# Two blanked triangles of turned p, written straight onto their partitions, and loads placed by fixed leads, in a two-layer decoder trunk

## The chip, the cores and the metric

The kernel runs on one core of one Trainium2 chip. The time is device microseconds (us) of one launch, the median of several runs. The engines are called PE (TensorE matmul; PEld is its weight load), DVE (VectorE), ACT (ScalarE), POOL (GpSimd) and SP (SyncE, which here only issues DMAs).

## The reference

Two decoder layers on x of 1024 tokens by 1024 channels, float32. Layer 0 mixes tokens with a short gated convolution, layer 1 with sliding-window attention; each is followed by a dense SwiGLU channel mixer.

```python
def reference(x, ...):
    for i in range(DEPTH):
        h = rmsnorm(x, norm_mixer[i])
        if i % N_MIXERS == 0:
            mix = short_conv_mixer(h, conv_w_in[j], conv_w[j], conv_w_out[j])
        else:
            mix = swa_sink_attention(h, attn_w_qkv[j], attn_q_gain[j], attn_k_gain[j], attn_sinks[j], attn_w_o[j])
        x = x + mix
        h = rmsnorm(x, norm_ffn[i])
        x = x + swiglu_ffn(h, ffn_w_gate_up[i], ffn_w_down[i])
    return x
```

The attention has 16 query heads and 4 key/value heads of 64 channels, with query and key normed for each head, a distance bias and a sink for each head. It works in blocks of 128 queries. A query at place q of its block sees the keys j <= q of its own block and the keys j > q of the block before: 128 keys in all, so that the two masks fit together like two triangles of one square.

## The kernel before

Activations lie with the channel on the partitions. Every product is made from float32r halves: an operand is split into a high part and the rest (a low part), and three matmuls (high by high, high by low, low by high) stand for one float32 product. So PE does three matmuls for each block of a product, and ACT and DVE split the operands.

**The order is written out by hand.** A `Line` holds PE's work in order; `line.work(n, f)` puts in work of n matmuls of 0.2265 us (`MM`), and `line.at(t, f)` places the work of the other engines at a time t on that same planned clock. `line.run()` then issues everything in the order of these times. Each engine, and SP's queue too, works off its own instructions strictly in that order, so an instruction that waits holds up all that stand behind it on its engine. The planned times set only the order; when things really run is decided by the semaphores.

**The attention** runs through 32 units u = 0 to 31: block b = u // 4, and within it one key/value head with its four query heads (QUAD). While unit u's scores are made, unit u - 1 is turned (transposed) and unit u - 2 is multiplied by v. On POOL stand, for each unit, the `normal` of p (L1931), the blanking (`select`), a difference of v (`dv_sum`, `dv_lo`) and the low parts of the output (`o_lo`). The steps that the change touches:

- `merge`, `bias`, `least`, `exponents`, `inverse`, `normal`: one square of scores for each head, own block where j <= q and the block before where j > q, then the softmax in the room `e_room`.
- `turn` (L1937): four transposes give p with the keys on the partitions. `turn_hi` (ACT, L1948) and `turn_lo` (DVE, L1952) put its high and low part into a room w (tag G0).
- `values` (L1972): both parts times a mixed v, whose partitions 0 to 63 hold the own block and 64 to 127 the block before.
- The mixed v is wrong for two triangles of the square: keys 0 to 63 with j > q (first half of the queries), and keys 64 to 127 with j <= q (second half). `other_values` (L1981) puts them right: it multiplies the difference of the two v's (`dv_room`) with these triangles alone. Each matmul has 128 partitions, 64 keys with the high part of p and the same 64 keys with the low part.
- `select` (POOL, L1957 and L1958) blanks all but the triangle with `affine_select`, for the high part (e = 0) and the low part (e = 1), into a second room o (tag G1). It leaves both parts of a triangle on the partitions that they came from. `under` (SP, L1962 and L1963) then copies two of the four pieces to the other 64 partitions with two DMAs inside SBUF, 64 partitions by 256 elements each.

Both rooms are single: `select` of one unit waits until `other_values` of the unit before has read o.

**What else is on SP's queue.** `key_twice` (L1782), `v_down` (L1795) and `dv_twice` (L1811, L1812) are small DMAs inside SBUF. From unit 24 on, PE's free places are filled with the output projection (`tail_part`, L1061 to L1063), tiles m = 0 to 7 of the first half of the tokens, eight pieces of three matmuls each, then the same for the second half. Each tile loads its `w_o`, which an earlier stage has split and stored (`wo_parts`), as two DMAs of 512 KB (L1035) into a pair of rooms; three pairs take turns (WR, WH, WL). `load_again` (L2209) brings the residual tiles X0 to X7 back from `xmid`, 512 KB each; the rooms have held query weights until unit 26. The residual add (L1086) needs X of a tile when the tile is done. From the sums of squares that follow come the means (L1103).

Where these loads stand before: `state["loads"]` keeps, for each unit, a time 5.1 us behind its start. The `wo` loads of a tile stand at the last of these marks that is at least 7 us ahead of the tile, or 15 us ahead of it if that is later. X0 stands at the start of unit 27, and one further X near the mark of each unit from 27 to 33.

Of the kernel before, what the change touches and what calls it, by code (L numbers as in the profile page):

```python
# [11 lines left out]
F32R = mybir.dt.float32r  # L12
AF = mybir.ActivationFunctionType
ALU = mybir.AluOpType

P = 128
# [4 lines left out]
HD = 64  # L21
# [11 lines left out]
QUAD = NH // NKV  # L33
# [37 lines left out]
def trunk_kernel(ctx: ExitStack, tc: tile.TileContext, xT, small, table, w_in, w_out, w_kv, w_q, w_o, w_gu, w_dn, out):  # L71
    nc = tc.nc
    sb = ctx.enter_context(tc.tile_pool(name="sb", bufs=1))
    pm = ctx.enter_context(tc.tile_pool(name="pm", bufs=1, space=bass.MemoryType.PSUM))
    dve, act, pool, pe = nc.vector, nc.scalar, nc.gpsimd, nc.tensor
# [3 lines left out]
    def slot(tag, shape=(P, D), dtype=F32, bufs=1):  # L79
        uid[0] += 1  # L80
        return sb.tile(list(shape), dtype, tag=tag, name=f"{tag}_{uid[0]}", bufs=bufs)
# [28 lines left out]
    def plain(ap):  # L110
        return ap.bitcast(F32)
# [125 lines left out]
    state = {}  # L237
# [550 lines left out]
    class Line:  # L788
# [8 lines left out]
        def at(self, t, f, *args):  # L797
            self.n += 1
            heapq.heappush(self.heap, (t, self.n, f, args))
# [205 lines left out]
    def channel_mixer(layer, next_stage, src_of, operands, raw_tags, extra_tags, slots, line, lead_in):  # L1005

        at = line.at
# [10 lines left out]
        def tail_weights(h, m, t):  # L1018
            it = {}

            def load():
                it["w"] = Weights()
                it["w"].load(src_of(m), 0, n_op)

            def hi():
                c = slice(0, n_op * P)
                it["w"].alloc()
                it["steps"] = split_steps(it["w"].hi[:, c], it["w"].lo[:, c], it["w"].raw[:, c])
                it["steps"][0]()

            def load_parts():
                tag = ("WR", "WH", "WL")[(NK * h + m) % 3]
                it["w"] = SimpleNamespace(hi=slot(tag, dtype=F32R, bufs=2), lo=slot(tag, dtype=F32R, bufs=2))
                for e, room in enumerate((it["w"].hi, it["w"].lo)):
                    nc.sync.dma_start(plain(room), wo_parts[m][e])  # L1035

            if layer == 1:
                at(max([b for b in state["loads"] if b < t - 7.0][-1], t - 15.0), load_parts)
            else:
                at(t - 14.0, load)  # L1040
                at(t - 5.2, hi)
                at(t - 4.2, lambda: it["steps"][1]())
            return lambda: (it["w"].hi, it["w"].lo)
# [113 lines left out]
        for u in range(GROUP):  # L1157
            if whole:
                t = (origin + 4.0, origin + 12.0, begin1 + 1.0, begin1 + 8.0)[u]
# [12 lines left out]
        t = begin1 + 6.2  # L1172
        for odd in (0, 1):
            if odd and whole:
                t = begin1 + 28.0
# [5 lines left out]
        t = begin2 + 6.2  # L1181
# [30 lines left out]
        t = begin2 + 20.5  # L1212
# [309 lines left out]
        for k in range(1, KINDS):  # L1522
            s = begin + GROUP * down * k
# [14 lines left out]
        for k in range(1, KINDS):  # L1538
            if k == KINDS - 1 and next_stage is not None:
                t = line.end  # L1540
# [4 lines left out]
        if layer == 0:  # L1545
            for i in range(2 * GROUP):
                u = i // 2
# [6 lines left out]
    def attention_layer(line, mixer):  # L1554
        at = line.at
# [80 lines left out]
        room = {}  # L1636
# [71 lines left out]
        def dv_room(b):  # L1708
            if ("dv", b % 2) not in room:
                room["dv", b % 2] = slot(("G10", "G3")[b % 2], (P, 2, NKV, 2, HD), F32R)  # L1710
            return room["dv", b % 2]
# [226 lines left out]

        def turn_rooms():
            if "PT" not in room:  # L1940
                room["PT"] = slot("G0", (P, 2, QUAD * P), F32R), slot("G1", (P, 2, 2, QUAD, HD), F32R)
            return room["PT"]

        def by_halves(x):
# [9 lines left out]
        def select(u, e):  # L1954
            w, o = turn_rooms()
            w = by_halves(w[:, e])
            pool.affine_select(o[0:HD, e, 0], w[0:HD, 0], [[0, QUAD], [-1, HD]], ALU.is_ge, 0.0, -1, 1)  # L1957
            pool.affine_select(o[:, e, 1], w[:, 1], [[0, QUAD], [1, HD]], ALU.is_ge, 0.0, HD, -1)  # L1958

        def under(u):  # L1960
            o = plain(turn_rooms()[1])
            nc.sync.dma_start(o[HD:P, 0, 0], o[0:HD, 1, 0])  # L1962
            nc.sync.dma_start(o[0:HD, 0, 1], o[HD:P, 1, 1])  # L1963

        def flat(x):
            return x.rearrange("p e d -> p (e d)")
# [10 lines left out]
        def other_values(u):  # L1977
            b, c, g = parts(u)
            ps = by_halves(S[u]["pv"])
            for i in (0, 1):  # L1980
                pe.matmul(  # L1981
                    ps[:, i], flat(dv_room(b)[:, i, 2 * c + g]), turn_rooms()[1][:, 0, i],
                    start=False, stop=i == 1, skip_group_check=True,
                )

# [32 lines left out]
        def lead_in(tail_part, tail_item):  # L2018
# [3 lines left out]
            t = line.end  # L2022
# [43 lines left out]
            for k in range(NK):  # L2066
# [4 lines left out]
                if k == NK - 2:  # L2071
                    t = line.end
# [28 lines left out]
            for u in range(24, 32):  # L2101
                fill[u] += [(tail_piece,)] * (6 - len(fill[u]))

            state["loads"] = []

            def unit(u, last):

                s = line.end
                state["loads"].append(s + 5.1)
                n, g = u // 2, u % 2  # L2110
                b, c = n // 2, n % 2
                todo = deque(fill[u] if u < NU else [])
# [50 lines left out]
                if 4 <= u - 1 < NU:  # L2163
                    t = max(line.end + 0.7, s + 4.0)
                    at(line.end + 0.1, select, u - 1, 0)
                    at(t, select, u - 1, 1)
                    at(t + 0.9, under, u - 1)
                if u >= NU:
                    for _ in range(6):
                        next_piece()  # L2170
# [3 lines left out]
                if n + 2 < 16 and g == 0:  # L2174
                    m = n + 2
# [33 lines left out]
                nc.sync.dma_start(X[m], xmid[m])  # L2209

            for u in range(NU + 2):
                if u == 27:
                    at(line.end, load_again, 0)
                unit(u, u == NU + 1)
                if u >= 27:
                    at(state["loads"][-1] + (2.6 if u == 28 else 0.1), load_again, u - 26)
            at(line.end - 3.0, open_ends)
            while tails:
                tail_piece()
# [116 lines left out]
```

## Time and profile before

| | |
|---|---|
| median of 3 runs | 1909.11 us (1906.8 to 1909.56) |
| the profiled execution | 1906.79 us, its span 1905.1 us |
| granted TensorE clock, mean | 0.999 of full speed |
| attention units 0 to 31 | from about 989 to 1202 us of the span |
| DMA inside SBUF by `under` | 56 transfers, 1025 to 1208 us |
| loads of `wo` | 32 transfers of 512 KB, 1136 to 1254 us |

The profile is of one execution. Its page gives busy times of the engines and the chain of work that ended last. The view of waits lists who waited for whom: microseconds in total, how many times, and the longest. The view by line groups instructions: out<-in by the program's names, shape, count, busy time, mean ns of one, and the idle time of the engine ahead of them with its releaser. A timeline row is start, duration, engine, line and operation, with the idle time ahead of it in brackets. SPq is SP's queue of DMA issues; a row of it is the issue, not the transfer. The rows of windows give busy time (and count) of PE, PEld, DVE, ACT and POOL in a stretch, then the granted clock, the busy share of the DMA engines and GB/s.

### The profile page before, as it was taken

How to read it: one execution, taken by the hardware profiler on the slowest of the kernel's cores; microseconds unless marked ns; L12 is line 12 of the kernel's file. 1: busy time of each engine (PE TensorE's matmuls, PEld its weight loads, DVE VectorE, ACT ScalarE, POOL GpSimd, SP SyncE). 2: the span in 40 equal slices, each digit the busy share in tenths (PEclk: the TensorE clock that was granted, in tenths of full speed). 3: DMA queues.
4: the chain of work that ended last, by engine and by line, in shares of the span. 5: the costliest groups of instructions: out<-in, count | busy, mean ns of one | idle time of the engine just before them, and what ended most of it. 6: DMA issues, size and time to landing. Idle time of an engine off the chain costs nothing.

```text
span 1905.1 us, 24998 instructions
## 1 busy us (share of the span) xinstructions
PE 1891.7 (99%) x8603; PEld 1568.5 (82%) x8603; DVE 1372.6 (72%) x2233; ACT 852.1 (45%) x1710; POOL 325.3 (17%) x634
## 2 busy tenths in 40 slices
PE   9999999999999999999999999999999999999998
PEld 7888888888888888888888887788888888888887
DVE  8997878867777777766678887468767676765553
ACT  5543444533333334444557776335333333344441
POOL 0000011012222221000016776300111111100000
PEclk9999999999999999999999999999999999999999
DMA  8522186156666667986731125844454654577562
GB/s 313 171 99 74 66 294 217 59 174 221 218 235 213 224 206 250 355 296 226 243 101 37 43 68 155 300 178 139 149 187 150 218 188 157 170 271 274 192 229 96
DMA packets 164736, 355.08 MB, mean 186 GB/s; under 512 B 16832, under 2 KB 64832, under 8 KB 164480
## 3 DMA queue, kind: packets, MB, share of 16 engines
q1 hardware_dynamic: 138112, 260.50, 41.2%
q0 software_dynamic: 26208, 92.81, 13.4%
q8 instruction: 68, 1.11, 0.2%
q14 instruction: 60, 0.49, 0.1%
q10 hardware_dynamic: 288, 0.16, 0.0%
HBM read 241.34 MB, written 103.28 MB: 181 GB/s over the span
## 4 chain that ended last, share of the span: by engine, by line
PE 96%; DMA 2%; DVE 1%; issue 1%; POOL 0%; ACT 0%; SPq 0%; DVEq 0%; POOLq 0%; ACTq 0%
PE acc L946 16%; PE acc L948 16%; PE acc L947 16%; PE P L946 9%; PE P L948 9%; PE P L947 9%; PE P L1653 2%; PE acc L1061 2%; PE acc L1063 2%; PE acc L1062 2%; PE P L1655 2%; PE P L1654 2%; PE twin L1888 1%; PE acc L175 1%; DMA G<-G 1%; PE acc L1937 1%
## 5 line engine op out<-in xcount | busy, mean ns | idle before, releaser
L946 PE MATMUL acc<-XS,G 128*128 128x512 f32 x880 | 342.5, 389 | 0.0
L948 PE MATMUL acc<-XS,G 128*128 128x512 f32 x880 | 342.4, 389 | 0.0
L947 PE MATMUL acc<-XS,G 128*128 128x512 f32 x880 | 342.3, 389 | 0.0
L948 PEld LDWEIGHTS acc<-XS,G 128*128 128x128 f32 x880 | 165.2, 188 | 34.4
L947 PEld LDWEIGHTS acc<-XS,G 128*128 128x128 f32 x880 | 165.2, 188 | 34.2
L946 PEld LDWEIGHTS acc<-XS,G 128*128 128x128 f32 x880 | 165.2, 188 | 34.1
L946 PE MATMUL P<-A,G 128*128 128x512 f32 x476 | 185.2, 389 | 0.0
L947 PE MATMUL P<-A,G 128*128 128x512 f32 x476 | 185.2, 389 | 0.0
L948 PE MATMUL P<-A,G 128*128 128x512 f32 x476 | 185.2, 389 | 0.0
L946 PE MATMUL acc<-A,G 128*128 128x512 f32 x441 | 171.7, 389 | 0.0
L948 PE MATMUL acc<-A,G 128*128 128x512 f32 x441 | 171.4, 389 | 0.0
L947 PE MATMUL acc<-A,G 128*128 128x512 f32 x441 | 171.4, 389 | 0.0
L882 DVE TENSOR_TENSOR G<-WL,G 128x512 fp32r<-128x512 f32 x168 | 117.1, 698 | 46.1 <-ACT G L881 46.1
L881 ACT CAST G<-WR 128x512 fp32r<-128x512 f32 (+1 forms) x200 | 120.9, 605 | 62.4 <-PE acc L948 30.5
L882 DVE TENSOR_TENSOR G<-WR,G 128x512 fp32r<-128x512 f32 (+1 forms) x200 | 134.5, 673 | 9.4 <-ACT G L881 9.1
L881 ACT CAST G<-WH 128x512 fp32r<-128x512 f32 (+1 forms) x158 | 94.9, 601 | 80.4 <-PE acc L948 37.9
L1232 ACT ACTIVATE G<-G 128x512 f32<-128x512 f32 x88 | 55.8, 634 | 159.8 <-DVE G L1303 155.7
L946 PE MATMUL P<-XS,G 128*128 128x512 f32 x316 | 123.0, 389 | 0.1
L947 PE MATMUL P<-XS,G 128*128 128x512 f32 x316 | 122.9, 389 | 0.0
L948 PE MATMUL P<-XS,G 128*128 128x512 f32 x316 | 122.9, 389 | 0.0
L881 ACT CAST G<-WL 128x512 fp32r<-128x512 f32 x168 | 103.6, 617 | 42.9 <-DVE WL L821 38.3
L882 DVE TENSOR_TENSOR G<-WH,G 128x512 fp32r<-128x512 f32 (+1 forms) x158 | 106.7, 675 | 7.6 <-ACT G L881 7.4
(335 smaller groups left out, 3819.0 us busy)
## 6 DMA issues: line engine op xcount, KB each, us to landing
G<-h SPq DMA_DIRECT2D x70, 512.0 KB, 5.1
h<-X POOLq DMA_DIRECT2D x44, 512.0 KB, 5.6
X<-in_w_dn SPq DMA_DIRECT2D x80, 256.0 KB, 3.5
s<-X POOLq DMA_DIRECT2D x40, 512.0 KB, 4.1
WR<-in_w_gu SPq DMA_DIRECT2D x36, 512.0 KB, 5.8
WH<-in_w_gu SPq DMA_DIRECT2D x36, 512.0 KB, 6.3
h<-X POOLq DMA_DIRECT2D x66, 256.0 KB, 3.6
WR<-s SPq DMA_DIRECT2D x54, 256.0 KB, 3.2
```

The lines of the kernel that those rows point to most:

```text
L881: lambda: act.copy(out_hi, raw),
L882: lambda: lo_eng.tensor_tensor(out_lo, raw, plain(out_hi), ALU.subtract),
L946: pe.matmul(ps[:, q], w[:, 0, c], x[:, 0, q], start=start and e == 0, stop=False, skip_group_check=True)
L947: pe.matmul(ps[:, q], w[:, 0, c], x[:, 1, q], start=False, stop=False, skip_group_check=True)
L948: pe.matmul(ps[:, q], w[:, 1, c], x[:, 0, q], start=False, stop=last, skip_group_check=True)
L1061: pe.matmul(ps, hi[:, kc], xs[:, 0, c], start=k == 0, stop=False, skip_group_check=True)
L1062: pe.matmul(ps, hi[:, kc], xs[:, 1, c], start=False, stop=False, skip_group_check=True)
L1063: pe.matmul(ps, lo[:, kc], xs[:, 0, c], start=False, stop=k == n_op - 1, skip_group_check=True)
L1232: state["silu"] = act.activation(x, x, AF.Silu)
L1653: pe.matmul(ps, x[:, 0, t], hi, start=k == 0, stop=False)
L1654: pe.matmul(ps, x[:, 0, t], lo, start=False, stop=False)
L1655: pe.matmul(ps, x[:, 1, t], hi, start=False, stop=k == NK - 1)
```

## The change

`select` now writes each blanked triangle where `other_values` reads it: the first triangle's high part to partitions 0 to 63 and its low part to 64 to 127, the second one's the other way round. So for e = 1 the output partitions differ from the input's by 64. `under` is gone with its DMAs, and o is half as large. The `wo` loads of a tile stand 13 us ahead of it, and the X loads stand in pairs: X0 and X1 at the start of unit 27, then two each 5.3 us into units 28, 29 and 30.

```diff
             if layer == 1:
-                at(max([b for b in state["loads"] if b < t - 7.0][-1], t - 15.0), load_parts)
+                at(t - 13.0, load_parts)
...
-                room["PT"] = slot("G0", (P, 2, QUAD * P), F32R), slot("G1", (P, 2, 2, QUAD, HD), F32R)
+                room["PT"] = slot("G0", (P, 2, QUAD * P), F32R), slot("G1", (P, 2, QUAD, HD), F32R)
...
         def select(u, e):
             w, o = turn_rooms()
             w = by_halves(w[:, e])
-            pool.affine_select(o[0:HD, e, 0], w[0:HD, 0], [[0, QUAD], [-1, HD]], ALU.is_ge, 0.0, -1, 1)
-            pool.affine_select(o[:, e, 1], w[:, 1], [[0, QUAD], [1, HD]], ALU.is_ge, 0.0, HD, -1)
-
-        def under(u):
-            o = plain(turn_rooms()[1])
-            nc.sync.dma_start(o[HD:P, 0, 0], o[0:HD, 1, 0])
-            nc.sync.dma_start(o[0:HD, 0, 1], o[HD:P, 1, 1])
+            for i, (first, slope) in enumerate(((-1, 1), (0, -1))):
+                rows, out = slice(i * HD, (i + 1) * HD), slice((i ^ e) * HD, ((i ^ e) + 1) * HD)
+                pool.affine_select(o[out, i], w[rows, i], [[0, QUAD], [-slope, HD]], ALU.is_ge, 0.0, first, slope)
...
-                    ps[:, i], flat(dv_room(b)[:, i, 2 * c + g]), turn_rooms()[1][:, 0, i],
+                    ps[:, i], flat(dv_room(b)[:, i, 2 * c + g]), turn_rooms()[1][:, i],
...
-            state["loads"] = []
-
             def unit(u, last):
 
                 s = line.end
-                state["loads"].append(s + 5.1)
...
                     at(line.end + 0.1, select, u - 1, 0)
                     at(t, select, u - 1, 1)
-                    at(t + 0.9, under, u - 1)
...
             for u in range(NU + 2):
-                if u == 27:
-                    at(line.end, load_again, 0)
+                if 27 <= u < 31:
+                    for m in (2 * u - 54, 2 * u - 53):
+                        at(line.end + (0.0 if u == 27 else 5.3) + 0.1 * (m % 2), load_again, m)
                 unit(u, u == NU + 1)
-                if u >= 27:
-                    at(state["loads"][-1] + (2.6 if u == 28 else 0.1), load_again, u - 26)
```

## The prediction

> **What bounds the kernel now.** First the page: the span, the engines' busy row, and the chain that ended last.
>
> ```profile
> span 1905.1 us, 24998 instructions
> PE 1891.7 (99%) x8603; PEld 1568.5 (82%) x8603; DVE 1372.6 (72%) x2233; ACT 852.1 (45%) x1710; POOL 325.3 (17%) x634
> PE 96%; DMA 2%; DVE 1%; issue 1%; POOL 0%; ACT 0%; SPq 0%; DVEq 0%; POOLq 0%; ACTq 0%
> ```
>
> TensorE is busy nearly throughout and its work isn't changed, so the edit can win only time in which PE stands still. The view of waits, for PE alone, says where that is:
>
> ```profile
> PE acc L1981 <- DMA G<-G: 5.3, 4, 2.7
> PE P L1103 <- DVE A L1090: 1.1, 1, 1.1
> ```
>
> L1981 is the pair of correction matmuls (`other_values`); the DMA it waits for is `under` (L1962, L1963), which the change deletes. These five waits, 6.4 us, are the prize. But a wait also costs the refill of a pipelined engine, so I price it from the starts of units in the chain (L1888 is a unit's first work; units 18, 20, ... 30):
>
> ```profile
> 1104.49 0.95 PE twin L1888 x8
> 1117.54 0.95 PE twin L1888 x8
> 1130.88 0.95 PE twin L1888 x8
> 1145.38 0.95 PE twin L1888 x8
> 1158.36 0.95 PE twin L1888 x8
> 1173.18 0.95 PE twin L1888 x8
> 1189.88 0.95 PE twin L1888 x8
> ```
>
> Three pairs of units run undisturbed: 13.05, 13.34 and 12.98, mean 13.12. The others take 14.50, 14.82 and 16.70, which is 1.4, 1.7 and 3.6 too much, together 6.65 us. The longest is in unit 29; the timeline of SP's queue, POOL and PE shows how it comes about:
>
> ```profile
> 1179.02 1.55 SPq L1035 DMA_DIRECT2D WR<-wo  x2
> 1179.23 0.41 POOL L1958 TENSOR_SCALAR_AFFINE_SELECT G<-G 128x256 fp32r<-128x256 f32 x1
> 1180.68 0.49 SPq L1962 DMA_DIRECT2D G<-G  x1
> 1186.53 0.59 PE L1981 MATMUL acc<-G,G 128*128 128x256 f32 x2 [2.75 <-DMA G<-G]
> ```
>
> POOL has blanked everything at 1179.64. SP is still issuing two weight loads; `under` follows them at 1180.68, and PE gets its data 5.85 us later. L1962 by itself:
>
> ```profile
> L1962 SPq DMA_DIRECT2D G<-G  x28: 461/467/545, 1025.3 to 1207.3; - x28
> DMA to landing us min/median/max: 1.9/1.9/5.8
> ```
>
> The median transfer lands in 1.9 us, and only one behind a bulk load takes up to 5.8. So 24 of the 28 units show no wait, and nothing is to be won before the weight loads of L1035 begin.
>
> **The change, part by part.**
>
> *The transfers go:* 28 times two DMAs, and PE then waits for the last select only. The first disturbed unit shows what room that leaves:
>
> ```profile
> 1136.64 0.41 POOL L1958 TENSOR_SCALAR_AFFINE_SELECT G<-G 128x256 fp32r<-128x256 f32 x1
> 1140.35 0.60 PE L1937 MATMUL acc<-cst,G 128*128 128x128 f32 x4
> ```
>
> The last select ends at 1137.05, and L1981 would follow L1937 at about 1140.7: 3.7 us to spare. I count the three waits of units 22 to 29 as removed, 6.65. The fourth at L1981 is what their 1.4, 1.7 and 3.6 don't hold; its own share of the 5.3 is at most a few tenths, and I take 0.2.
>
> *The selects are rewritten.* There are still four for a unit, of 256 elements a partition, but those of the second part (two for a unit, 56 in all) read partitions 0 to 63 and write 64 to 127, or the other way. No row of before shows POOL doing that. The nearest rows, from the groups by line:
>
> ```profile
> L1957 POOL TENSOR_SCALAR_AFFINE_SELECT G<-G 64x256 fp32r<-64x256 f32 x56 | 23.0, 411 | 30.4 <-ACT G L1948 11.8 <-DVE G L1952 10.8 <-PE acc L1981 7.1
> L1958 POOL TENSOR_SCALAR_AFFINE_SELECT G<-G 128x256 fp32r<-128x256 f32 x56 | 23.0, 410 | 0.0
> L1856 DVE TENSOR_TENSOR G<-P,G 64x512 fp32r<-64x512 f32 x26 | 17.9, 689 | 5.5 <-ACT G L1852 5.1
> L1952 DVE TENSOR_TENSOR G<-acc,G 128x512 fp32r<-128x512 f32 x29 | 20.1, 692 | 5.3 <-POOL XS L2015 2.7 <-ACT G L1948 1.7
> ```
>
> Half as many partitions cost POOL the same (411 against 410 ns), so nothing is won by the narrower form. VectorE's L1856 writes other partitions than it reads, and takes no longer (689) than the straight L1952 (692). So I take nothing for the shift. The lower end is nothing too: no fewer instructions and no fewer elements for a partition. As the upper end I take twice the time, as if the two halves went one after the other: 0.82 for 0.41, or 0.82 us more for a unit. Not all of POOL is covered:
>
> ```profile
> PEld acc L1937 <- POOL G L1931: 2.4, 8, 0.4
> 1126.15 1.03 POOL L1931 TENSOR_TENSOR G<-G,at_d 128x512 f32<-128x512 f32 x1
> 1127.24 0.66 PE L1937 MATMUL acc<-cst,G 128*128 128x128 f32 x4
> ```
>
> `normal` (L1931) stands behind the selects in POOL's queue, and here the transposes (L1937) start 0.06 us after it ends; in 8 units PE's weight load really waits for it, 0.3 each. Longer selects would reach PE in such units. That is the slower rival below.
>
> *The X loads move.* By the planner's clock (0.2265 us a matmul, units of 6.1 to 6.6 us) X0 stays at the start of unit 27 and X1 comes right behind it; X2 moves up by 2.4 us, X3 and X4 by about 6, X5 and X6 by 12, X7 by 19. Each is one DMA of 512 KB on SP, moved past several pairs of `wo` loads. The price of the old place:
>
> ```profile
> 1218.39 1.05 SPq L1035 DMA_DIRECT2D WR<-wo  x2
> 1219.49 0.42 SPq L2209 DMA_DIRECT2D X<-xmid  x1
> 1227.02 0.69 DVE L1086 TENSOR_TENSOR X<-P,X 128x512 f32<-128x512 f32 x1 [6.26 <-DMA X<-xmid]
> 1210.00:1230.00 20.00, 18.57 (x85) 14.80 (x84) 4.85 (x7) 3.37 (x8) 3.54 (x7) 1.00 0.95 321
> ```
>
> X7 is issued behind a `wo` pair that waited for its buffer, lands 7.5 us later on engines that are 95% busy, and holds up the residual add, the squares, and the means at L1103. Issued some 19 us sooner it is there in time: 1.1 us won.
>
> *The `wo` loads* go out 13 us ahead of use. By the planner those of tiles 0 and 2 hardly move, 3 gains 3.9 us, and the others of the first half 1.9 to 2.7, except that 7, like the second half, still waits in SP's queue for its buffer (three sets of rooms and 5.4 us of matmuls a tile: a set comes free two tiles, 10.9 us, ahead of use). Behind that wait stand only later loads of this kind and the first gate-up loads, which need nothing for some 10 us. I count zero; the cover is that PE waits for no `wo` load in before, and without it a late pair would cost some 7 us, as X7's load does above.
>
> *What is late next.* X0, which doesn't move, is the weak spot. The timeline of units 27 and 28:
>
> ```profile
> 1164.02 0.91 SPq L1035 DMA_DIRECT2D WL<-wo  x2
> 1164.94 1.11 PE L1888 MATMUL twin<-G,G 128*128 128x256 f32 x8
> 1166.21 0.58 SPq L2209 DMA_DIRECT2D X<-xmid  x1
> 1171.12 0.69 DVE L1086 TENSOR_TENSOR X<-P,X 128x512 f32<-128x512 f32 x1 [1.75 <-DMA X<-xmid]
> 1173.01 1.11 PE L1888 MATMUL twin<-G,G 128*128 128x256 f32 x8
> 1175.63 1.03 POOL L1931 TENSOR_TENSOR G<-G,at_d 128x512 f32<-128x512 f32 x1
> 1176.72 0.66 PE L1937 MATMUL acc<-cst,G 128*128 128x128 f32 x4
> ```
>
> L1086 waits for X0 and starts 6.18 us into unit 27. Behind it in VectorE's queue stands the low part of turned p, behind that POOL's second selects, behind these `normal` and then PE's transposes: from 1171.12 to 1176.66, 5.54 us of back-to-back work. Without `under` ahead of it X0 is issued 1.3 us sooner, but the same `wo` pair is still moving, and I give it 0.6. So `normal` ends 11.1 us after the start of unit 27. PE, no longer held, starts unit 28 at 6.2 instead of 8.07 and wants the transposes 3.7 later, at 9.9: a wait of 1.2 us comes back. For unit 30, where PE also gains on POOL, I put one more ordinary wait of 0.3.
>
> *Sum:* 6.65 + 0.2 + 1.1 − 1.2 − 0.3 = 6.45 us. The profiled execution took 1906.79 (span 1905.1 and 1.7 around it): 1900.3. It is the fastest of the runs shown, whose median is 1909.11, and the same gain from there gives 1902.7. The removed waits depend on when transfers land and may be larger in those runs, so I forecast the middle, **1901.5**.
>
> **The rivals.**
>
> *Loads crowd each other.* X1 right behind X0, and X2 and X3 ahead of the last SBUF transfers of `dv_twice`. If X0 shares the engines with X1, 0.52 MB more at the 321 GB/s above, it lands 1.6 us later, and so does unit 28; for `dv_twice` behind two X loads I put 2 us. The gain falls to 6.45 − 3.6 = 2.85, time 1905.1 on the same basis. For it: DMA is near full wherever loads bunch. Against it: they are issued in turn on one queue, and fewer of them fall into the crowded 20 us.
>
> *The wait changes its name only.* PE waits for the last select as long as it did for the DMA, and only X7's 1.1 is won: 1906.9. Against it speak the 3.7 us to spare.
>
> *Shifted selects are slow: slower than before.* At twice the time a unit's POOL chain is 0.82 longer. The loss lies between 8 × 0.82 = 6.6 (only where PE's weight load waits already) and 28 × 0.82 = 23.0 (no cover anywhere); in the middle 14.8, against 6.45 won: 1901.5 + 14.8 = 1916.3. With 18 units exposed, it decides from 6.45 / 18 = 0.36 a unit, a shifted select of 0.59 us instead of 0.41. For it: no shifted POOL row. Against it: the four rows above.
>
> [...]
>
> **How the numbers follow.** Forecast 0.70, crowded loads 0.15, renamed wait 0.04, slow shift 0.08, quarter of POOL 0.03. About 0.2% (3.8 us) is what a measurement of this kernel can tell from no change, so faster begins below 1905.3. The forecast lies there but for 0.04 (the before time scatters by 2.8 us itself), and of the crowded loads 0.06. Faster 0.66 + 0.06 = 0.72, same 0.04 + 0.09 + 0.04 = 0.17, slower 0.11. The range begins where all 7.95 us are won from the fast profiled run and nothing comes back, with half a microsecond of scatter, 1898.3, so 1898. Above it takes in the crowded loads and the renamed wait, and of the unknown shift all up to the point from which it decides, 1907.5. Its full ends are the 0.11 left out.
>
> **What would show it.** Right: no wait of PE at L1981; none at L1103; the pairs of units from 22 on at about 13.1 us, but the one with unit 27 up to 1.2 longer, waiting for `normal`; shifted selects at 0.41. Wrong: PE waiting at L1937 in most units (slow selects), a DMA among the releasers in units 27 to 31 (crowded loads), or L1981 waiting for POOL.

## The result, and the profile after

| | before | changed |
|---|---|---|
| median of 7 runs, us | 1909.04 (1906.8 to 1913.69) | 1902.45 (1901.56 to 1905.01) |
| profiled execution, its span, us | 1906.79, 1905.1 | 1902.64, 1900.9 |
| mean granted clock, profiled execution | 0.999 | 1.0 |

The ratio is 0.9966, with an interval of 0.9955 to 0.9978: 6.6 us less in the medians, a third of a per cent. The forecast was 1901.5. The two profiled executions differ by less, 4.15 us. Which of the two numbers the mechanism accounts for is the question of this section and of the experiments.

The page of the changed kernel has the same 8603 matmuls, but the chain of work that ended last is no longer nearly all PE's: it passes through POOL, DVE and ACT now.

```profile
PE 1891.5 (100%) x8603; PEld 1567.9 (82%) x8603; DVE 1372.0 (72%) x2233; ACT 852.2 (45%) x1710; POOL 330.4 (17%) x634
PE 90%; POOL 3%; DVE 3%; ACT 2%; issue 1%; DMA 1%; SPq 0%; DVEq 0%; POOLq 0%; ACTq 0%
```

The view of waits for PE and its weight load has no row for the correction matmuls (`other_values`, now L1977) and none for the means (L1103). In their place the transposes wait for `normal`: the weight load 14 times, 6.7 us, where it was 8 times and 2.4.

```profile
PE acc L1937 <- POOL G L1931: 1.8, 5, 0.8
PE twin L1888 <- DVE G L1856: 0.9, 1, 0.9
PEld acc L1937 <- POOL G L1931: 6.7, 14, 1.3
```

The chain still begins units 18, 22, 26 and 30 with L1888, but in between the transposes now hang on POOL's `normal`, as here in unit 21, ahead of unit 22:

```profile
1127.68 1.01 POOL G L1931
1128.74 0.66 PE acc L1937 x4
1132.38 0.95 PE twin L1888 x8
```

From the first L1888 of each unit in the timelines, the time between unit starts splits the difference of the two profiles into places:

| stretch | before, us | changed, us | difference | forecast |
|---|---|---|---|---|
| units 6 to 22, no bulk load under way | 105.89 | 107.18 | +1.3 | 0 |
| units 22 to 24 | 14.49 | 13.11 | −1.4 | −1.4 |
| units 24 to 26 | 12.98 | 13.52 | +0.5 | 0 |
| units 26 to 28 | 14.82 | 13.12 | −1.7 | −1.7 |
| units 28 to 30 | 16.70 | 16.39 | −0.3 | −3.6 + 1.5 |
| unit 30 to the means | 39.49 | 37.85 | −1.6 | −1.3 |

Together −3.2, and −3.0 at the means (1229.20 before, 1226.21 after) with 0.2 of scatter ahead of unit 6. Another 1.3 us come from the very end: the last output store ends the span 2.9 us after its issue here, and 4.2 us in the profile of before. A second profile of the kernel before (below) has 2.9 too, so these 1.3 us are scatter and no gain. The units 22 to 24 and 26 to 28 went as forecast. Two things did not: a loss in the undisturbed units, and units 28 to 30, which gave nearly all of their gain back. The timeline of units 27 and 28 shows the latter:

```profile
1165.75 0.85 SPq L2201 DMA_DIRECT2D X<-xmid  x2
1165.77 1.12 PE L1888 MATMUL twin<-G,G 128*128 128x256 f32 x8
1171.74 0.69 DVE L1086 TENSOR_TENSOR X<-P,X 128x512 f32<-128x512 f32 x1 [1.54 <-DMA X<-xmid]
1173.30 0.94 PE L1888 MATMUL twin<-G,G 128*128 128x256 f32 x6 [0.93 <-DVE G L1856]
1176.51 1.03 POOL L1931 TENSOR_TENSOR G<-G,at_d 128x512 f32<-128x512 f32 x1
1177.60 0.66 PE L1937 MATMUL acc<-cst,G 128*128 128x128 f32 x4 [0.28 <-POOL G L1931]
...
1184.89 0.66 PE L1937 MATMUL acc<-cst,G 128*128 128x128 f32 x4 [0.85 <-POOL G L1931]
```

X0 lands late, the residual add waits 1.54 us for it, and the low part of turned p, the selects, `normal` and the transposes follow in a row. Unit 28 starts at 1171.97 and has its transposes 5.63 us later, where before they came 3.71 after its start. This is the chain of the prediction, in its place, but longer: 1.9 us are lost, 0.9 of them at the unit's first matmuls already, for which VectorE was late. In unit 29 the transposes wait another 0.85 for POOL.

The stretch ahead of the means, in the window that the prediction showed of the kernel before:

```profile
1210.00:1230.00 20.00, 20.00 (x97) 16.71 (x96) 6.53 (x14) 4.30 (x11) 3.68 (x8) 1.00 0.72 257
```

PE is busy throughout, and the DMA engines 72% instead of 95%.

### The profile page after: what moved, and what is told of

Its sections match the earlier page's. It is cut to its first block, busy times and chain, and to the rows that moved or that the text cites. A ratio compares the mean times of both kernels' runs of the same rounds, so it can differ in the third digit from the quotient of the medians.

```text
span 1900.9 us, 24865 instructions
## 1 busy us (share of the span) xinstructions
PE 1891.5 (100%) x8603; PEld 1567.9 (82%) x8603; DVE 1372.0 (72%) x2233; ACT 852.2 (45%) x1710; POOL 330.4 (17%) x634
## 4 chain that ended last, share of the span: by engine, by line
PE 90%; POOL 3%; DVE 3%; ACT 2%; issue 1%; DMA 1%; SPq 0%; DVEq 0%; POOLq 0%; ACTq 0%
PE acc L946 16%; PE acc L947 16%; PE acc L948 16%; PE P L946 9%; PE P L947 9%; PE P L948 9%; PE acc L1061 2%; PE acc L1062 2%; PE acc L1063 2%; PE acc L175 1%; PE P L1653 1%; PE P L1655 1%; PE P L1654 1%; POOL G L1959 1%; POOL G L1931 1%
```

## The experiments

Each kernel is compared with runs of the kernel before on the same chip. The medians of these comparison runs lie between 1908.41 and 1910.24, so a difference of 1 or 2 us between the medians of two experiments needs its timeline beside it. The theory at the outset: the direct selects take away the waits for transfers, POOL's chain and X0 give part of it back. The rivals: the loads bring the gain, or the loads cost something, or the shifted selects do.

**1. The selects alone.** The changed kernel with the loads at their old places.

```diff
-                at(t - 13.0, load_parts)
+                at(max([b for b in state["loads"] if b < t - 7.0][-1], t - 15.0), load_parts)
...
-                if 27 <= u < 31:
-                    for m in (2 * u - 54, 2 * u - 53):
-                        at(line.end + (0.0 if u == 27 else 5.3) + 0.1 * (m % 2), load_again, m)
+                if u == 27:
+                    at(line.end, load_again, 0)
                 unit(u, u == NU + 1)
+                if u >= 27:
+                    at(state["loads"][-1] + (2.6 if u == 28 else 0.1), load_again, u - 26)
```

> The changed kernel with the load places of before (wo at the marks, one X for each unit), so the direct selects and the missing SBUF transfers alone. If the deleted transfers carry the gain: no wait at L1981's place, the wait at the means stays (1.1 us in the profile of before), and the time is about 1904, 1.5 us over the changed kernel. If the earlier loads carry it: 1907 or more.

Measured: 1903.17 us, ratio 0.9970 (0.9959 to 0.9982). Nearly the whole gain is there. The waits of PE have nothing at the correction matmuls, and a rest at the means:

```profile
PE P L1103 <- DVE A L1090: 0.3, 1, 0.3
```

**2. The loads alone.** The kernel before, with the selects and `under` as they were, and the loads of the change: the same edit the other way round.

```diff
-                at(max([b for b in state["loads"] if b < t - 7.0][-1], t - 15.0), load_parts)
+                at(t - 13.0, load_parts)
...
-                if u == 27:
-                    at(line.end, load_again, 0)
+                if 27 <= u < 31:
+                    for m in (2 * u - 54, 2 * u - 53):
+                        at(line.end + (0.0 if u == 27 else 5.3) + 0.1 * (m % 2), load_again, m)
```

> The kernel before with the new places of the loads, the SBUF transfers left in. If the transfers are what PE waits for, they still queue behind the loads: waits of PE for the SBUF transfers of 4 us or more stay, the wait at the means goes, time 1906 to 1909. If the earlier loads carry the gain: about 1903, with hardly a wait for the transfers.

Measured: 1911.23 us, ratio 1.0010 (1.0001 to 1.0019). The wait at the means is gone, but the transfers inside SBUF now stand behind more loads:

```profile
PE acc L1981 <- DMA G<-G: 7.9, 6, 2.5
```

So the new places of the loads are no gain of their own; where the transfers still exist they cost a little (the interval begins just above 1). Two waits of 1.20 and 1.37 us are new, at 1209 and 1217 us, and in both places `under` follows a pair of `wo` loads on SP's queue. In the changed kernel they are worth 1903.17 − 1902.45 = 0.7 us, within the scatter of both.

**3. X0 earlier.** The changed kernel, with X0 issued in unit 26 instead of at the start of unit 27.

```diff
+                if u == 26:
+                    at(line.end + 2.4, load_again, 0)
                 if 27 <= u < 31:
                     for m in (2 * u - 54, 2 * u - 53):
-                        at(line.end + (0.0 if u == 27 else 5.3) + 0.1 * (m % 2), load_again, m)
+                        if m:
+                            at(line.end + (0.0 if u == 27 else 5.3) + 0.1 * (m % 2), load_again, m)
```

> The changed kernel with X0 alone issued 2.4 us into unit 26, ahead of the wo pair of tile 2. If the late X0 holds up the chain of residual add, low part of turned p, second selects and normal: VectorE waits no longer for X0, the transposes of unit 28 come near 3.7 us after its start instead of 5.6, and the time falls by about 2 us to 1900.5. If only POOL's longer selects hold unit 28 up: the same time within 0.5 us.

Measured: 1900.71 us, ratio 0.9958 (0.9945 to 0.9970), 1.74 below the changed kernel. In its timeline the residual add of tile 0 no longer waits, and unit 28, which starts at 1172.15, has its transposes 3.94 us later:

```profile
1170.24 0.68 DVE L1086 TENSOR_TENSOR X<-P,X 128x512 f32<-128x512 f32 x1
1176.09 0.66 PE L1937 MATMUL acc<-cst,G 128*128 128x128 f32 x4 [0.28 <-POOL G L1931]
```

Units 28 to 30 take 14.72 instead of 16.39. So the late X0 costs the changed kernel 1.7 us. The transposes still wait for POOL, though.

**4. The wide select again.** The second select of the high part, which isn't shifted, in its old form of 128 partitions.

```diff
+                if i and not e:
+                    pool.affine_select(o[:, 1], w[:, 1], [[0, QUAD], [1, HD]], ALU.is_ge, 0.0, HD, -1)
+                    continue
```

> The changed kernel with the second select of the high part in the form of before, 128 partitions from 0 (the second part overwrites the half that is too much). If a select that starts at partition 64 costs 0.1 us on each side, as the spacing of starts in the trace suggests (0.95 us for a pair against 0.75 before): the first pair of a unit falls back to about 0.75, POOL has 0.2 us less for each unit, and the time falls by 0.5 to 1.5 us. If the pair is slower for another reason (waits between selects, the smaller room): spacing stays at 0.95 and the time as it is.

Measured: 1902.0 us, ratio 0.9965 (0.9953 to 0.9977). The first pair of a unit did become 0.2 us shorter, from 0.95 to 0.73, but the time went down by 0.45 only, within the scatter and just short of the 0.5 to 1.5 expected, and units 6 to 22 take 107.07 us against 107.18. The reason is in POOL's timeline of this kernel (L1959 is the wide select here, L1962 the others): after the first pair POOL idles for 1.05 us until the second pair's data come, so hardly anything but the second pair's length reaches `normal`.

```profile
1130.07 0.41 POOL L1962 TENSOR_SCALAR_AFFINE_SELECT G<-G 64x256 fp32r<-64x256 f32 x1
1130.44 0.41 POOL L1959 TENSOR_SCALAR_AFFINE_SELECT G<-G 128x256 fp32r<-128x256 f32 x1
1130.80 0.18 POOL L1908 COPY G<-cst 128x4 f32<-128x4 f32 x1
1132.03 0.87 POOL L1962 TENSOR_SCALAR_AFFINE_SELECT G<-G 64x256 fp32r<-64x256 f32 x2 [1.05 <-DVE G L1952]
```

**5. `normal` ahead of `o_lo`.** Kernel 3, with the low parts of the output 1.5 us later on the planned clock, which puts them behind `normal` in POOL's queue.

```diff
-                            at(s + 6.5 + 5.0, o_lo, n - 1, (0, 1))
-                            at(s + 13.0 + 5.0, o_lo, n - 1, (2, 3))
+                            at(s + 6.5 + 6.5, o_lo, n - 1, (0, 1))
+                            at(s + 13.0 + 6.5, o_lo, n - 1, (2, 3))
```

> X0 early as in the run before, and besides the low parts of the output (o_lo, two of 0.46 us for a unit) placed 1.5 us later, so that POOL does normal ahead of them. If PE's transposes now wait on POOL's chain of second selects, difference of v, o_lo and normal: the waits of PE's weight load for normal (6.4 us in 14 units) nearly vanish, the units of the stage run at the 13.05 us a pair of the planner or less, and the time falls by 1.5 to 2.5 us, to about 1898.5. If the transposes wait for something else (exponents, the reciprocal): no change, 1900.7.

Measured: **1896.57 us** (1896.43 to 1896.8), ratio 0.9935 (0.9922 to 0.9948), the fastest kernel of this study, and below both times of its expectation. PE's waits in the attention are down to one, and 98% of the chain is PE's again. The one wait, and the starts of units 18, 20, 22, 24, 26, 28 and 30 in the chain:

```profile
PE acc L1937 <- POOL G L1931: 0.4, 1, 0.4
```

```profile
1104.04 0.95 PE twin L1888 x8
...
1117.02 0.95 PE twin L1888 x8
...
1130.24 0.95 PE twin L1888 x8
...
1143.22 0.95 PE twin L1888 x8
...
1156.37 0.95 PE twin L1888 x8
...
1169.36 0.95 PE twin L1888 x8
...
1183.19 0.95 PE twin L1888 x8
```

that is 12.98, 13.22, 12.98, 13.15, 12.99 and 13.83 us apart. Two of the three pairs that the prediction called undisturbed in the kernel before (13.05, 13.34, 12.98) were thus about 0.1 us longer than they had to be.

**6. The second pair twice.** The shifted selects are issued two times over, with the same result: some 0.95 us more of POOL in each unit.

```diff
-                pool.affine_select(o[out, i], w[rows, i], [[0, QUAD], [-slope, HD]], ALU.is_ge, 0.0, first, slope)
+                for _ in range(1 + e):
+                    pool.affine_select(o[out, i], w[rows, i], [[0, QUAD], [-slope, HD]], ALU.is_ge, 0.0, first, slope)
```

> The changed kernel with the second pair of selects (low part of turned p, shifted by 64 partitions) issued twice in each of the 28 units: 0.95 us more on POOL for a unit, the price of the slower rival made real. In the changed kernel normal ends 0.05 us ahead of the transposes in most units, so if POOL's chain is what sets the pace there, nearly all of it shows: 28 x 0.95 less the little room left is 22 us, time about 1924. If POOL still has cover (as the prediction's middle, 18 units, had it): 17 us or less, about 1919. If the transposes wait for other engines: under 5 us.

Measured: 1916.62 us, ratio 1.0038 (1.0025 to 1.0051), 14.2 above the changed kernel. Waits in its profile:

```profile
PE acc L1937 <- POOL G L1931: 15.3, 26, 1.7
```

28 units by 0.95 are 26.6 us of POOL, so each microsecond more in the second pair costs 0.53 us of time. The chain through the selects binds, with about half of it covered. At this rate the 0.82 us a unit of the rival of slow selects would have cost 12.2 us; the rival put 14.8, with 18 of 28 units exposed, which was somewhat too dear but of the right size.

**7. The kernel before, once more**, unchanged, for a second profile.

> The kernel before once more, for a second profile of it. If the profiled execution of before was a lucky one (its 1906.8 against a median of 1908.4 to 1909.1), this one shows longer waits of PE for the SBUF transfers, 7 to 8 us in all, and the rest of the span is the same. If its time differs for another reason (the last stores, the start): the waits stay at 5 to 6 us and the difference stands elsewhere.

Measured: 1908.06 us, a span of 1905.9 us. Up to unit 28 it is the first profile within 0.1 us. Then units 28 to 30 take 18.99 instead of 16.70. The wait in unit 29 comes in two pieces here, one for each of the two transfers, together 3.3 us instead of 2.75, and what follows it is slower:

```profile
1186.41 0.39 PE L1981 MATMUL acc<-G,G 128*128 128x256 f32 x1 [2.59 <-DMA G<-G]
1187.47 0.58 PE L1981 MATMUL acc<-G,G 128*128 128x256 f32 x1 [0.67 <-DMA G<-G]
...
1188.28 0.63 PE L1062 MATMUL P<-XS,WL 128*128 128x512 f32 x1
1188.70 0.63 PE L1063 MATMUL P<-XS,WL 128*128 128x512 f32 x1
```

The matmuls start 0.42 us apart. The windows of this profile give the granted clock, third number from the end:

```profile
1186.00:1188.00 2.00, 0.92 (x3) 0.72 (x4) 0.69 (x1) 0.00 (x0) 0.41 (x1) 0.87 0.94 260
1188.00:1190.00 2.00, 2.00 (x7) 1.52 (x6) 0.69 (x1) 1.89 (x8) 1.88 (x6) 0.50 0.11 43
```

In the first profile the same stretch runs at full clock, with 12 matmuls in the middle window instead of 7:

```profile
1188.00:1190.00 2.00, 2.00 (x12) 1.68 (x11) 0.73 (x3) 2.00 (x12) 1.84 (x5) 1.00 0.25 78
```

So in this profile the last wait of the kernel before is followed by a lower TensorE clock. The clock stays at 0.50 for 3.41 us, from 1187.47 on, which costs 1.7 us of the 2.3; the rest is the longer wait. In these 3.41 us matmuls of 512 columns start 0.42 to 0.43 us apart, and 0.23 apart in the same work of the first profile, at full clock. What brings the clock down the traces do not show. It fell after waits of 3.3 (here) and 4.0 us (kernel 11), and not after 2.75 in the first profile, but it also fell in kernel 8 (further below). There X0 came late, PE had waited 1.40 and 0.41 us, and it was busy for 1.62 of the 3.41 us ahead of the drop, as the windows of that kernel show:

```profile
1171.51:1174.92 3.41, 1.62 (x9) 1.36 (x10) 3.29 (x7) 2.17 (x9) 1.85 (x4) 1.00 0.23 88
1174.92:1178.33 3.41, 3.41 (x13) 2.74 (x11) 2.05 (x4) 2.30 (x8) 2.11 (x4) 0.50 0.54 147
```

How often this happens can be read, roughly, from the runs, each of which gives its mean granted clock. All runs of the kernel before that stand beside the experiments, by that clock:

| mean granted clock | 1.0 | 0.999 | 0.998 | 0.997 | 0.996 |
|---|---|---|---|---|---|
| runs | 3 | 22 | 15 | 12 | 2 |
| median, us | 1905.50 | 1908.18 | 1909.67 | 1910.86 | 1913.95 |

One drop of 3.41 us at half clock lowers this mean by 0.0009. The profiles also show a low clock after PE's last matmul, where it costs nothing; within the span it lowers the mean by up to 0.0008, and the first profile, at 0.999, has that alone. If the other runs are like the profiled ones, a run at 1.0 had no drop, a run at 0.999 one or none, and the 29 of 54 runs at 0.998 or less had at least one. Of the 7 runs of the changed kernel 6 have a clock of 1.0, and their median is 1902.4. At full clock the change is thus worth some 3.1 us (three runs on one side), what the two profiles show up to the means. The other half of the 6.6 us goes with the lower clock, and with the somewhat longer waits ahead of it (3.3 us in this profile against 2.75 in the first); this rests on the table and on two profiles of the kernel before, not on a run in which the clock alone was changed.

**8 and 9. What the shift costs.** In the changed kernel the two selects of a pair, from the first's start to what follows the second, take 0.95 to 0.96 us, and in the kernel before 0.73 (first pair) to 0.76 (second pair). Before, the second pair:

```profile
1130.69 0.41 POOL L1957 TENSOR_SCALAR_AFFINE_SELECT G<-G 64x256 fp32r<-64x256 f32 x1 [1.12 <-DVE G L1952]
1131.06 0.41 POOL L1958 TENSOR_SCALAR_AFFINE_SELECT G<-G 128x256 fp32r<-128x256 f32 x1
1131.45 0.73 POOL L1788 TENSOR_TENSOR G<-G 128x256 f32<-128x256 f32 x1
```

After, the first pair of the same unit, which isn't shifted, and its groups by line:

```profile
1130.16 0.89 POOL L1959 TENSOR_SCALAR_AFFINE_SELECT G<-G 64x256 fp32r<-64x256 f32 x2
1131.12 0.19 POOL L1908 COPY G<-cst 128x4 f32<-128x4 f32 x1
```

```profile
L1959 POOL TENSOR_SCALAR_AFFINE_SELECT G<-G 64x256 fp32r<-64x256 f32 x112 | 47.0, 420 | 23.8 <-ACT G L1948 9.9 <-DVE G L1952 9.4
```

The mean of one select hardly moves (411 and 410 to 420 ns); the 0.2 us lie in the distance from start to start. And the unshifted pair has them too, so the shift isn't the cause. Two kernels that take and put the triangles in other places (their output is another one) separate the possibilities: in the first all four selects read partitions 0 to 63, and the second pair writes 64 to 127; in the second all read 64 to 127, and the second pair writes 0 to 63.

```diff
-                rows, out = slice(i * HD, (i + 1) * HD), slice((i ^ e) * HD, ((i ^ e) + 1) * HD)
+                rows, out = slice(0, HD), slice(e * HD, (e + 1) * HD)
```

```diff
-                rows, out = slice(i * HD, (i + 1) * HD), slice((i ^ e) * HD, ((i ^ e) + 1) * HD)
+                rows, out = slice(HD, P), slice((1 - e) * HD, (2 - e) * HD)
```

> A probe of what a select costs: every select reads partitions 0 to 63; the first pair writes 0 to 63, the second 64 to 127. The sums of the correction are left out by that (wrong triangles). If it is the read from partition 64 on that costs 0.1 us: both pairs fall back to about 0.75 from start to next start. If it is the write to 64 on: the first pair 0.75, the second 0.95. If it is two instructions of 64 partitions in a row, whatever their place: both stay at 0.95.

> The counterpart: every select reads partitions 64 to 127; the first pair writes 64 to 127, the second 0 to 63 (again other triangles than wanted). If the read from partition 64 on costs: both pairs 0.95 or a little less, for two in a row of the same place. If the write to 64 on costs: the first pair 0.95, the second 0.75. If only the change from one place to the other costs: both pairs about 0.75 to 0.85.

Measured, POOL's timeline of the first kernel (a pair without shift, then a pair with it), then of the second:

```profile
1115.89 0.78 POOL L1959 TENSOR_SCALAR_AFFINE_SELECT G<-G 64x256 fp32r<-64x256 f32 x2 [0.40 <-ACT G L1948]
1116.62 0.18 POOL L1908 COPY G<-cst 128x4 f32<-128x4 f32 x1
...
1117.75 0.78 POOL L1959 TENSOR_SCALAR_AFFINE_SELECT G<-G 64x256 fp32r<-64x256 f32 x2 [0.94 <-DVE G L1952]
1118.61 0.74 POOL L1792 TENSOR_TENSOR G<-G,G 128x256 f32<-128x256 f32 x1
```

```profile
1116.31 0.78 POOL L1959 TENSOR_SCALAR_AFFINE_SELECT G<-G 64x256 fp32r<-64x256 f32 x2 [0.39 <-POOL at_y L1692]
1117.16 0.19 POOL L1908 COPY G<-cst 128x4 f32<-128x4 f32 x1
```

Two selects with the same partitions on each side take 0.78 together, shifted or not: 0.37 from start to start and 0.41 for the last. In the changed kernel, where a pair goes from one half of the partitions to the other, it is 0.89. To an instruction that starts at partition 0 the low pair needs 0.73, the high pair 0.85 and the shifted pair 0.86. These numbers fit one reading: an instruction on POOL starts about 0.1 us later when its first partition, read or written, differs from that of the instruction ahead of it, and the shift as such costs nothing.

The semaphores in the traces' records say more, and the reading above is not the whole of it. In the changed kernel 63 of the instructions right behind a select wait for a semaphore that only POOL itself counts up, that is, for POOL's own earlier work, and all of them start 0.47 to 0.50 us after that select's start. Selects that start 0.37 apart overlap, since each takes 0.41; such a wait ends the overlap. In kernel 6 the same select follows itself on the same partitions, and starts 0.48 apart, with such a wait. So in most places the 0.1 us goes with a wait that the program sets, with or without a change of partitions. One case is left that waits for nothing: the second of the two shifted selects in the changed kernel, which swap halves, starts 0.46 us after the first all the same, in 27 of 28 units. Why, no view shows.

The times are one run each (1902.63, with the clock drop shown under 7, and 1900.66), too few for a difference of that size; units 6 to 22 take 106.66 and 106.61 us, between the kernels before (105.89) and after (107.18).

**10. `normal` first, X0 as it was.** The edit of kernel 5 on the changed kernel, so that POOL's chain and X0 are told apart.

```diff
-                            at(s + 6.5 + 5.0, o_lo, n - 1, (0, 1))
+                            at(s + 6.5 + 6.5, o_lo, n - 1, (0, 1))
...
```

> The changed kernel with o_lo behind normal, X0 where the change puts it. If the two repairs are for two separate losses (X0 late in unit 27, POOL's chain in the units before): the gain of o_lo is 3 to 4 us here too, 1898.5 to 1899.5, and a wait in unit 28 stays. If o_lo behind normal also takes the late X0 off the path: 1896.6, as with both.

Measured: 1898.18 us, ratio 0.9943 (0.9931 to 0.9955), 4.3 below the changed kernel. With the 1.7 of kernel 3 that makes 6.0, and kernel 5, which has both, has 5.9: two separate losses. PE still waits in unit 28 for what X0 holds up:

```profile
PE twin L1888 <- DVE G L1856: 0.7, 1, 0.7
```

**11. The same on the kernel before**, to see if its selects were hidden.

```diff
-                            at(s + 6.5 + 5.0, o_lo, n - 1, (0, 1))
+                            at(s + 6.5 + 6.5, o_lo, n - 1, (0, 1))
...
```

> The kernel before with o_lo behind normal, nothing else. If POOL's chain of second selects, o_lo and normal set the pace before as well (11 of 27 units with 0.06 us between normal and the transposes): the undisturbed pairs fall from 13.1 to 13.0 and the time by 1 to 1.5 us, the waits for the SBUF transfers stay. If the chain set the pace only in the changed kernel, with its 0.4 us more of POOL for a unit: no change.

Measured: 1909.57 us, ratio 1.0002 (0.9993 to 1.0012): nothing. Yet units 5 to 23 take 0.9 us less (117.84 against 118.71). The wait in unit 29 swallowed it, and a lower clock followed: in the profile of this kernel the granted clock is 0.50 for 3.41 us from 1186.58 on.

```profile
1186.25 0.76 PE L1981 MATMUL acc<-G,G 128*128 128x256 f32 x2 [4.00 <-DMA G<-G]
```

PE comes sooner and the transfer does not, so the wait grows from 2.75 to 4.00. A gain ahead of a transfer that decides when PE goes on is no gain.

**12. One number.** The kernel before, with the mark of the bulk loads 1.6 us later, so that SP issues `under` ahead of them. The transfers stay, and so do the selects.

```diff
-                state["loads"].append(s + 5.1)
+                state["loads"].append(s + 6.7)
```

> The kernel before, selects and SBUF transfers as they were, with one number changed: the marks at which wo and X loads stand lie 6.7 us into a unit instead of 5.1. SP then issues the transfers of a unit ahead of the bulk loads of that unit, and in unit 27 X0 ahead of the wo pair of tile 2. If PE waits for the transfers only because they queue behind a bulk load just issued: the three waits of units 23, 27 and 29 vanish, no clock falls, and the time is 1902 to 1904, that of the changed kernel, without its selects. If the transfers are late under any bulk load in flight, or the chain over POOL is what counts: waits of 3 us or more stay, 1906 or more.

Measured: 1902.48 us, ratio 0.9960 (0.9947 to 0.9974), the same as the whole change. SP's queue and the waits of PE in this kernel:

```profile
1177.56 0.48 SPq L1962 DMA_DIRECT2D G<-G  x1
...
1180.29 1.11 SPq L1035 DMA_DIRECT2D WR<-wo  x2
```

```profile
PE acc L1981 <- DMA G<-G: 0.8, 3, 0.4
```

The weight loads now stand behind the transfer, and of the 5.3 us of waits 0.8 are left. The transfers themselves cost little; their place behind a load just issued was the cost. X0, too, stands ahead of its `wo` pair here, and the residual add of tile 0 doesn't wait for it.

## Why the forecast came out right, point by point

- **PE bounds, and only the waits for transfers late in the attention can be won.** Right. No wait is left at the correction matmuls or at the means; kernel 1 has nearly all the gain without the loads, and kernel 12 has it without the selects.
- **6.65 for units 22 to 29, 0.2 and 1.1 after.** Right where it can be read alone: 1.38 and 1.70 for the first two pairs against 1.4 and 1.7, and 1.64 for the stretch up to the means against 1.3. The three waits by themselves are 1.11, 1.28 and 2.75 us, 5.1 together; the 1.5 us by which the units are longer still is what the prediction calls the refill, and of a pipeline the trace of before shows that matmuls of 0.39 us start 0.23 us apart where PE doesn't wait. But in the last stretch the source was another one than forecast. Kernel 1, with X7 at its old place, already takes 38.31 us there (39.49 before, 37.85 changed): 1.2 of the 1.6 came with the deleted transfers, and the earlier loads, which were given 1.1, brought about 0.5.
- **Nothing for the shifted selects.** This step failed. The prediction compared durations, and those did stay: 420 ns, and a shift costs nothing in itself (kernels 8 and 9). It did not look at the distance from one start to the next, which was 0.37 us in the timeline of before, less than a select's 0.41: an overlap that could be lost. The four selects of a unit take 0.4 us longer together; kernel 4 shows that hardly more than the second pair's 0.2 reaches PE. In the profiles that is 1.3 us over units 6 to 22. Of the 0.5 in units 24 to 26 it is a part at most, for kernel 12, with the selects of before, also has 13.29 there against 12.98 and 13.52. The cover that the prediction named for the transposes, 0.06 us, was the place to see it. The rival of slow selects had this mechanism, and set 0.36 us a unit as the point from which it decides; measured 0.2 on the path it takes a share and not the whole.
- **1.2 back through X0 in unit 28, 0.3 through POOL.** The mechanism was right, and for the 1.2 its place too; both terms were too small: units 28 to 30 exceed 13.1 by 3.3 us instead of 1.5. Unit 28 starts 6.2 us into unit 27 (1165.77 to 1171.97), as forecast. The residual add was given 5.6 and came at 6.0; from there to the end of `normal` were given 5.54, and it took 5.8 (1171.74 to 1177.54). Together `normal` ends 11.8 instead of 11.1 us into unit 27, and the 1.2 became 1.9. The 0.3 became 0.85, in unit 29 and not in unit 30. Taken away by itself, X0 gives 1.7 (16.39 to 14.72 in kernel 3), and with `normal` ahead of `o_lo` as well 13.83 are left (kernel 5).
- **Nothing for the earlier `wo` loads.** Within the scatter (0.7 us, kernel 1 against the changed kernel).
- **Crowded loads.** Something like it exists: kernel 2 has 7.9 us of waits for the transfers inside SBUF instead of 5.3, though it doesn't tell a shared engine from a place behind a load in the queue. The change takes away those transfers in the same step, so most of the rival had no hold here. One part of it has: the residual add starts 6.0 us after X0's issue with X1 right behind it, and 4.9 after it in the profile of before (1166.21 to 1171.12), which is 1.1 of the 1.6 us that the rival had for X0. But X1 need not be the cause. From the issue of the `wo` pair ahead of X0 to the residual add it is 7.0 us in the changed kernel (1164.75 to 1171.74) and 7.1 in the kernel before (1164.02 to 1171.12), where no X1 follows; this suggests that X0 lands when the pair ahead lets it, and that issuing it sooner behind the same pair wins little. X1 alone wasn't tried: in kernel 1, too, it is issued right behind X0.
- **Quarter of POOL, 0.03.** Not so: no run shows a select that has a part of POOL alone. The 112 selects of the changed kernel take 420 ns on average, where those of before took 411 and 410, and in kernel 8 two shifted ones start 0.37 us apart.
- **From the sum to the median.** The prediction took the sum from the profiled 1906.79 and from the median 1909.11, and settled on the middle. The two profiles differ by 3.0 us up to the means where 6.45 were summed, so the forecast came out right by two errors that cancel: about 3.5 us of returned time it had not counted (1.3 + 0.5 + 1.8 in the table), and about as much that the removed waits are worth more in most runs. The latter it allowed for only as "may be larger". That these two came out alike was luck. The second profile of before (kernel 7) and the clocks of 54 runs point to the clock for the second: as read under kernel 7, it was halved for some microseconds in at least 29 of the 54 runs of the kernel before, and not in 6 of the 7 runs of the changed kernel.

What stays open: why the second shifted select starts 0.46 us after the first where it waits for nothing; what exactly brings the clock down; and whether kernel 12 with `normal` moved ahead, which has neither shifted selects nor transfers behind loads, would beat kernel 5. That wasn't tried.

## What to carry to other kernels

When PE waits for a small transfer, look first at what stands ahead of it in the same queue: moving the bulk load behind it (one number) gave as much as removing 56 transfers. Compare spacing from start to start, not durations, when an instruction's operands change place, and look for the short chain behind it: a 0.06 us gap between `normal` and the transposes meant that about half of every microsecond more on POOL was paid, and that a reordering there was worth 4.3 us in the changed kernel. One profile of a kernel with long waits may be a lucky one: the list of runs with their granted clocks tells whether others ran at a lower clock (29 of the 54 runs of the kernel before at 0.998 or less, the first profile at 0.999).

## What the runs showed of the hardware

- Two selects of 64 partitions by 256 elements on the same partitions start 0.37 us apart in kernel 8, whether or not they write 64 partitions away from where they read; with a wait for POOL's own earlier work ahead of the second instruction it was 0.47 to 0.50 (63 cases in the changed kernel), and the two selects that swap halves started 0.46 apart without one (27 of 28).
- A wait of PE of 3.3 us, one matmul within it, or of 4.0 us was followed by matmuls 0.42 us apart at a granted clock of 0.50; one of 2.75 us was not. Yet in kernel 8 a drop followed waits of 1.40 and 0.41 us. Each of these three drops (kernels 7, 8 and 11) lasted 3.41 us, which is 1.7 us of lost matmul time.
- The last output store ended the span 2.9 us after its issue in two profiles and 4.2 in a third, 1.3 us that have nothing to do with the change.
